# Seven-product groups summed in four PSUM banks, and 40 of 240 convolution taps on ScalarE with accumulating DMAs

## The chip, the cores and the metric

One NeuronCore of a Trainium2 chip runs the whole layer as one program. Its engines run side by side, each through its own list of instructions in order: TensorE (PE, matmuls into PSUM), VectorE (DVE), ScalarE (ACT) and GpSimd (POOL) for elementwise work, SyncE (SP) for issuing DMAs. Semaphores tie them together. An accumulating DMA, one that adds its source to its destination, is issued from POOL. The metric is the device time of one execution in microseconds (us), as the median of a few runs; less is better.

## What is computed

A decoder layer on x of 512 tokens by 2048 channels, f32:

```
h = rms_norm(x, g);  z = h @ W_in            # W_in: 2048 x 7168
a_val, a_glu, a_gate, q, k, v, b_gate = split(z)   # 1024 columns each
u = a_val * sigmoid(a_glu)
u = causal_depthwise_conv(u, w, b)           # 31 taps on 1024 channels
u = silu(layer_norm(u)) @ W_pw + b_pw
y_a = u * silu(a_gate)
o = dilated_window_attention(rms(q), rms(k), v)    # 16 heads of 64, three patterns
y_b = o * silu(b_gate)
out = x + concat(y_a, y_b) @ W_out           # W_out: 2048 x 2048
```

The convolution is, for each channel, `sum_j w[j] u[t - 30 + j] + b`. With d = 30 - j as the distance, there are 31 taps; d = 0 and the bias are one operation, so 30 remain for each of eight blocks of 128 channels: 240 taps.

## The kernel before

**Products.** A weight block is not multiplied in f32. ACT writes a scaled f16 high half and DVE the f16 remainder, and PE takes three f16 matmuls (`tri`, L409 to L413: high by high, high by low, low by high). The weights come in groups of 512 columns (L47): four groups of value and gate columns interleaved ("vg"), then q, k, v, the two gates, the pointwise projection and W_out. Each group has four raw tiles `wf` of 1 MB, loaded by SP into a ring of 8 (`RING`).

**Seven products.** For three groups (`SEVEN`, L53: vg 3, q 0, v 0) a 2 x 2 block product is formed with seven block products in place of eight, in Winograd's form of Strassen's scheme. `input_products` (L1106) writes such a group as a plan: a list of (sub-slot, action). It has 28 sub-slots of one half product each (4 k-tiles x 3 matmuls x 256 columns = 12 matmuls), and PE's matmuls for product n, k-half `pair`, row half m stand at sub-slot 4n + 2 pair + m. The sums of weight blocks s1 to s4 are formed in place in the raw tiles (`add`, L1116): s1 by DVE, s2, s3 and s4 by accumulating DMAs from POOL (`BY_DMA`, L55; the issue is L1122). `hi` (L1126, ACT, recorded at L1128) writes a product's high half `ws` five sub-slots ahead of its product, `lo` (L1130, DVE) the low half four ahead. The sums t1 to t4 of the activations are made beforehand in `sum_x` (L361). Each of the seven results has a PSUM bank of its own while it lives (`lin_ps`, four banks); they are joined on DVE (`first_block`, `joint`, `fifth`, `sixth`, `final`), with two or three results copied to SBUF by ACT first (`copy`, L1178), into tiles `cb`.

**Slots and order.** The order of all engines' instructions is written out by the program, not by a scheduler: a clock `clock[0]` counts slots, `after(n, fn)` puts an action n slots later, and each engine executes what was written to it in that order. A plain group takes 32 slots, 16 products of 4 k-tiles in two halves each; a seven-group uses 28 of its 32. vg 3 has slots 96 to 127, q 0 128 to 159, k 0 160 to 191, v 0 192 to 223, bg 0 224 to 255.

**The convolution.** `conv` (L537) is a generator, pair after pair of channel blocks. For each block ACT writes `cv` = u * w[30] + b (L544), and DVE adds the taps one by one with a fused multiply-add on 128 x 511 down to 128 x 482 elements. `run_conv` (L853) is called every slot: DVE's written work is counted by the helper class `Weighed` (L74; DVE's operations are recorded at its line, L80), a pace (`PACE`, 1230, and 1480 once attention has begun) is taken off per slot, and while the count is below zero the next taps are written. After the last tap the layer norm follows, whose column sums PE does (L568).

**The pool `slots`.** f32 tiles of 128 x 512 (u, cv, cb, gates and others) come from one pool of 35 buffers (`SLOTS`, L31). Who takes a buffer waits until its last users are done, DMAs among them.

**POOL** also computes small per-column scales: `esc` (L424), the scale with which a group's products leave PSUM, and `ss` in `norm_qk` (L470), the norm of q and k for each head.

Of the kernel before, what the change touches and what calls it, by code (L numbers as in the profile page):

```python
# [31 lines left out]
LP = 4  # L32
WARM = 9
# [5 lines left out]
PACE = 1230  # L39
# [15 lines left out]
BY_DMA = ("s2", "s3", "s4")  # L55
SUM_FROM = 58
SUM_STEP = 10
PACE_2 = 1480
# [12 lines left out]
class Weighed:  # L71
# [5 lines left out]
    def __getattr__(self, name):  # L77
        def call(out, src, *args, **kw):
            self.load += START + max(math.prod(a.shape[1:]) for a in (out, src) if hasattr(a, "shape"))
            return getattr(self.engine, name)(out, src, *args, **kw)  # L80
        return call
# [3 lines left out]
def layer(ctx: ExitStack, tc: tile.TileContext, xt, w1, w2, w3, g_in, conv_w, conv_b,  # L85
# [233 lines left out]
    H = S // 2  # L319
# [39 lines left out]
    xn, tx = {}, {}  # L359

    def sum_x(j):  # L361
# [5 lines left out]
        to = tx[j] = (wide if j < 4 else att).tile([P, 4, 2, H], F16, name="tx", tag="wide" if j < 4 else "att")  # L367
        V.tensor_sub(t1, b11, b12)
        V.tensor_sub(t3, b12, b22)
        V.tensor_add(t2, b22, t1)  # L370
        V.tensor_sub(t4, b21, t2)
        both = lambda t: t.rearrange("p (n t) -> p n t", n=2)

        def high():
            for n, t in ((0, t12), (2, t34)):
                A.activation(to[:, n:n + 2, 0], both(t), AF.Copy)

        def low():
            for n, t in ((0, t12), (2, t34)):
                V.tensor_tensor(to[:, n:n + 2, 1], both(t), to[:, n:n + 2, 0], op=OP.subtract)  # L380
# [28 lines left out]
    def tri(ps, a, b, first, last):  # L409
        (ah, al), (bh, bl) = a, b  # L410
        T.matmul(ps, ah, bh, start=first, stop=False)  # L411
        T.matmul(ps, ah, bl, start=False, stop=False)  # L412
        T.matmul(ps, al, bh, start=False, stop=last)  # L413
# [53 lines left out]

    by_head = lambda t: t.rearrange("p (h d) -> p h d", d=DH)

    def norm_qk(store, z, sq, n, to):  # L470
# [4 lines left out]
        def reduce():  # L475
            V.reduce_sum(ss, by_head(sq), axis=AX.X)
            f = 2.0 ** (-2 * QK_SHIFT)
            G.tensor_scalar(ss, ss, f / DH, f * RMS_EPS, op0=OP.mult, op1=OP.add)
            rsqrt(ss)
# [4 lines left out]
        def high():  # L484
            got["hl"] = temp("qhl", F16, [P, 2, S])
            A.activation(got["hl"][:, 0], z, AF.Copy)

        def low():
            hl_t = got["hl"]
            V.tensor_tensor(hl_t[:, 1], z, hl_t[:, 0], op=OP.subtract)  # L490
            for part in range(2):
                if store not in qk:
                    qk[store] = [wide_tile("qk4", [P, 4, S], F16) for _ in range(2)]
                to(qk[store][part], hl_t[:, part])
# [6 lines left out]
    def evac_qk(half_i, t, ps, is_k):  # L501
# [10 lines left out]
        if is_k and ("v", half_i) in SEVEN:  # L512
            n = [4 + 5 * (t > 0), 10 + 2 * t + 2 * (t > 0), 11 + 2 * t + 2 * (t > 0), 13 + 2 * t + 2 * (t > 0)]
        norm_qk(("k" if is_k else "q", half_i), z, sq, n,
                lambda to, src: nc.sync.dma_start(to[:, :, t * P:(t + 1) * P], src, transpose=True))
# [20 lines left out]

    def conv():  # L537

        for i0 in range(0, 8, 2):
            while i0 + 1 not in u:  # L540
                yield 1
            for i in (i0, i0 + 1):
                cv[i] = slot("cv")
                A.activation(cv[i], u[i], AF.Identity, scale=cw[:, i, TAPS - 1:TAPS], bias=cb[:, i:i + 1])  # L544
            yield 2
            for j in range(TAPS - 2, -1, -1):
                d = TAPS - 1 - j
# [151 lines left out]
    def two_heads(pair):  # L699
# [9 lines left out]
        def scores(tiles):  # L709
# [9 lines left out]
            for i in order:  # L719
                w = WIDTH[i]  # L720
                for n, (q, k) in enumerate(((0, 0), (0, 1), (1, 0))):
                    for a, rows in enumerate(halves):
                        T.matmul(ps[i, a], qk["q", hf][q][rows, p4, i * P:w], qk["k", hf][k][rows, p4, :w], start=n == 0, stop=n == 2)  # L723
# [126 lines left out]
    convolution = conv()  # L850
    wait = [0, False]

    def run_conv():  # L853

        pace = PACE_2 if 0 < min(at_pair.values(), default=0) <= clock[0] else PACE
# [249 lines left out]

    def input_products(i0):  # L1106
# [5 lines left out]
        def block(name, pair):  # L1112
            b = PLACE.get(name, name)
            return raw[i0 + 2 * pair + (b[2] == "2")][:, :, H * (b[1] == "2"):][:, :, :H]

        def add(name, pair):  # L1116
            if name == "s1":
                V.tensor_tensor(block("a11", pair), block("a22", pair), block("a11", pair), op=OP.subtract)
            else:
                x, to = SUMS[name]  # L1120
                if name in BY_DMA:
                    nc.gpsimd.dma_start(block(to, pair), block(x, pair), accum_op=OP.add)  # L1122
                else:
                    V.tensor_tensor(block(to, pair), block(to, pair), block(x, pair), op=OP.add)
# [5 lines left out]
        def lo(name, pair):  # L1130
# [3 lines left out]
            for j in range(4):  # L1134
                mine = ("s2", "s4") if j % 2 else ("s1", "s3")
                if all((n, j // 2) in done for n in mine) and all(m in free for m in range(j)) and j not in free:
# [3 lines left out]
                    after(MEASURE, lambda j=j: measure(i0 + j + RING))  # L1140

        def x_part(name, pair, k):

            if name[0] == "t":
                t = tx[4 * pair + k][:, int(name[1]) - 1]
# [4 lines left out]
        order = [("p1", "a11", "b11"), ("u", "a22", "t4"), ("x", "a12", "b21"), ("p7", "s3", "t3"), ("p5", "s1", "t1"),  # L1150
                 ("p6", "s2", "t2"), ("z", "s4", "b22")]
        u_first = group != SEVEN[0]
        if u_first:
            order[:2] = order[1::-1]

        def product(n, pair, m):
            to, w, x = order[n]
            if (pair, m) == (0, 0):
                bank[to] = lin_ps.tile([P, 2, H], F32, name="ps_l", tag="ps_l")
            ps, ms = bank[to][:, m], slice(m * P, (m + 1) * P)  # L1160
            for k in range(KU):
                t, xs = weights[w, pair], x_part(x, pair, k)
                first, last_ = pair == m == k == 0, pair == m == 1 and k == KU - 1
                if by_token:
                    tri(ps, [x[:, ms] for x in xs], (t[:, 0, k], t[:, 1, k]), first, last_)
                else:
                    tri(ps, [t[:, j, k, ms] for j in range(2)], xs, first, last_)
# [10 lines left out]
        def copy(name):  # L1178
            t = got[name] = slot("cb")
            A.activation(t, bank.pop(name).rearrange("p m t -> p (m t)"), AF.Copy, scale=e["p"])  # L1180
# [274 lines left out]
```

## Time and profile before

| | |
|---|---|
| median of 3 runs | 817.66 us (817.63 to 818.33) |
| span of the profiled execution | 815.8 us |
| PE busy | 807.9 us, 99% |
| DVE busy | 707.1 us, 87% |
| ACT busy | 553.6 us, 68% |
| POOL busy | 138.1 us, 17% |
| granted TensorE clock | 0.999 |
| moved by DMA | 125.62 MB, mean 154 GB/s |

A row of the groups reads: line, engine, operation, output tile <- input tiles, shapes, count | busy us, mean ns of one | idle time of the engine just before, and who released it. A row of waits reads: engine, tile and line <- the releaser: us in total, times, longest us. A DMA row gives count, KB each and the median us from issue to landing. The profile was taken from one execution, and the time of a run also holds what lies outside the span, 1.9 us between this span and the median.

### The profile page before, as it was taken

The numbers are of one execution on the slowest core, as the hardware profiler recorded it, in microseconds if no ns is written. First come the engines' busy times: TensorE is split into PE (matmuls) and PEld (weight loads), VectorE is DVE, ScalarE is ACT, GpSimd is POOL, SyncE is SP. The second block draws the span as 40 slices with busy tenths as digits, with TensorE's granted clock in tenths as the row PEclk, the third lists the DMA queues.
The fourth block names the chain that finished last, engine by engine and source line by source line (L and its number), as shares of the span: only waits on it lengthen the run. The fifth ranks groups of instructions, "written<-read, shape, count | busy, mean of one in ns | idle before, by whom it ended". The sixth has DMA issues, their size and how long they took to land.

```text
span 815.8 us, 13495 instructions
## 1 busy us (share of the span) xinstructions
PE 807.9 (99%) x5271; PEld 500.6 (61%) x5271; DVE 707.1 (87%) x1181; ACT 553.6 (68%) x778; POOL 138.1 (17%) x159
## 2 busy tenths in 40 slices
PE   9999999999999999999999999999999999999998
PEld 6887645888646864444444444444444444788887
DVE  6768999889888989999999988996677798998985
ACT  6667687567656678677756748487688858766540
POOL 0001020413223500004112010010110002412420
PEclk9999999999999999999999999999999999999999
DMA  9953343995675862537473632536343477578752
GB/s 341 344 215 102 105 110 98 132 279 113 261 143 114 156 252 98 122 104 174 136 181 100 172 105 86 134 104 168 104 117 104 136 236 234 116 176 189 130 104 66
DMA packets 98625, 125.62 MB, mean 154 GB/s; under 512 B 62720, under 2 KB 83968, under 8 KB 89344
## 3 DMA queue, kind: packets, MB, share of 16 engines
q1 hardware_dynamic: 80800, 107.38, 41.9%
q0 software_dynamic: 17472, 17.30, 14.9%
q8 instruction: 41, 0.67, 0.3%
q14 instruction: 24, 0.20, 0.1%
q10 hardware_dynamic: 288, 0.07, 0.0%
HBM read 88.56 MB, written 4.19 MB: 114 GB/s over the span
## 4 chain that ended last, share of the span: by engine, by line
PE 69%; DVE 19%; ACT 5%; issue 3%; DMA 3%; POOL 1%; SPq 0%; ACTq 0%; DVEq 0%; POOLq 0%
PE ps_l L411 17%; PE ps_l L412 17%; PE ps_l L413 16%; PE ps_l L879 10%; DVE cv L80 6%; DVE wl L80 3%; DVE ws L80 3%; ACT junk L190 2%; PE ps_s L413 2%; PE ps_s L411 2%; PE ps_s L412 2%; PE ps_s L723 2%; PE ps_o L763 2%; DMA wf<-w_dram 1%; DVE cb L80 1%
## 5 line engine op out<-in xcount | busy, mean ns | idle before, releaser
L80 DVE SCALAR_TENSOR_TENSOR cv<-u,cw,cv 128x511 f32<-128x511 f32 (+14 forms) x240 | 162.2, 728 | 0.4 <-ACT cv L544 0.4
L190 ACT ACTIVATE junk<-wf 128x2048 uint8<-128x2048 f32 x68 | 129.2, 1900 | 3.5 <-DMA wf<-w_dram 3.1
L411 PE MATMUL ps_l<-x,wh 128*128 128x512 f16 x320 | 121.4, 379 | 0.3 <-DVE glu L80 0.3
L413 PE MATMUL ps_l<-x,wl 128*128 128x512 f16 x320 | 121.3, 379 | 0.0
L412 PE MATMUL ps_l<-x,wh 128*128 128x512 f16 x320 | 121.3, 379 | 0.0
L299 ACT ACTIVATE wh<-wf,ws 128x2048 f16<-128x2048 f32 x44 | 87.7, 1993 | 49.0 <-PE ps_l L412 49.0
L80 DVE SCALAR_TENSOR_TENSOR wl<-wf,ws,wh 128x2048 f16<-128x2048 f32 x45 | 105.6, 2347 | 13.0 <-ACT wh L299 13.0
L411 PE MATMUL ps_l<-wh,x 128*128 128x512 f16 x256 | 97.1, 379 | 0.0
L412 PE MATMUL ps_l<-wl,x 128*128 128x512 f16 x256 | 97.1, 379 | 0.0
L413 PE MATMUL ps_l<-wh,x 128*128 128x512 f16 x256 | 97.0, 379 | 0.0
L80 DVE SCALAR_TENSOR_TENSOR ws<-wf,ws 128x1024 f16<-128x1024 f32 x70 | 89.0, 1278 | 7.5 <-ACT ws L1128 4.9
L411 PEld LDWEIGHTS <-wh 128*128 128x128 f16 x480 | 47.0, 98 | 55.4 <-issue 3.5
L413 PEld LDWEIGHTS <-wl 128*128 128x128 f16 x480 | 46.9, 98 | 53.6 <-DVE wl L80 0.4
L412 PEld LDWEIGHTS <-wh 128*128 128x128 f16 x480 | 46.9, 98 | 50.4 <-issue 0.7
L879 PE MATMUL ps_l<-xr,wr 128*128 128x512 f32 x288 | 69.7, 397 | 0.1
L204 POOL TENSOR_SCALAR ws<-ws 128x1 f32<-128x1 f32 x22 | 10.7, 485 | 341.8 <-DVE ws L80 313.0
L879 PEld LDWEIGHTS ps_l<-xr,wr 128*128 128x128 f32 x288 | 54.1, 189 | 13.8 <-ACT xr L338 1.0
L413 PEld LDWEIGHTS <-x 128*128 128x128 f16 x352 | 34.4, 98 | 32.8 <-issue 1.5
L411 PEld LDWEIGHTS <-x 128*128 128x128 f16 x352 | 34.4, 98 | 32.4 <-issue 1.9
L412 PEld LDWEIGHTS <-x 128*128 128x128 f16 x352 | 34.4, 98 | 30.6 <-issue 0.5
L946 ACT ACTIVATE ws<-wf,ws 128x1024 f16<-128x1024 f32 x28 | 32.1, 1147 | 28.7 <-PE ps_l L413 9.4
L1128 ACT ACTIVATE ws<-wf,ws 128x1024 f16<-128x1024 f32 x42 | 46.4, 1138 | 6.1 <-PE ps_l L413 3.9
(250 smaller groups left out, 1823.3 us busy)
## 6 DMA issues: line engine op xcount, KB each, us to landing
wf<-w_dram SPq DMA_DIRECT2D x72, 1024.0 KB, 5.2
wf<-wf POOLq DMA_DIRECT2D x30, 512.0 KB, 6.5
x<-xt_dram SPq DMA_DIRECT2D x16, 256.0 KB, 6.7
res<-xt_dram SPq DMA_DIRECT2D x8, 512.0 KB, 6.5
out_dram<-res SPq DMA_DIRECT2D x15, 256.0 KB, 2.2
wf<-w_dram SPq DMA_DIRECT2D x7, 512.0 KB, 7.2
wf<-wf POOLq DMA_DIRECT2D x6, 256.0 KB, 6.3
qk<-qhl SPq DMA_TRANSPOSE x40, 3.0
```

Of the source, the lines that this page charges most:

```text
L80: return getattr(self.engine, name)(out, src, *args, **kw)
L190: A.activation(junk[:, :n], src, AF.Square, scale=scale, accum_out=acc)
L204: G.tensor_scalar(scale, scale, 1e-30, 2.0 ** (-2 * top), op0=OP.max, op1=OP.mult)
L299: A.activation(parts[i][0], raw[i], AF.Copy, scale=wscale[units[i][3:]][0])
L411: T.matmul(ps, ah, bh, start=first, stop=False)
L412: T.matmul(ps, ah, bl, start=False, stop=False)
L413: T.matmul(ps, al, bh, start=False, stop=last)
L723: T.matmul(ps[i, a], qk["q", hf][q][rows, p4, i * P:w], qk["k", hf][k][rows, p4, :w], start=n == 0, stop=n == 2)
L763: T.matmul(po[rows, i * P:(i + 1) * P], vs[hf][j // 2][:, j % 2, 2 * p4 + a, vp * DH:(vp + 1) * DH], got["t", a][:, pp * (ALL // P) + FROM ...
L879: T.matmul(banks[group, m], wt[:, a, m * P:(m + 1) * P], xk[b], start=k == 0 and a == b == 0, stop=k == KC - 1 and a == 1)
L946: A.activation(t[:, 0], block(name), AF.Copy, scale=wscale["wa", g][0])
L1128: A.activation(t[:, 0], block(name, pair), AF.Copy, scale=wscale[group][0])
```

## The change

**Seven products.** The order of the products is new, and results that are only ever added are summed in one PSUM bank by PE itself. `ORDER` names the bank (A to D), the weight block or sum and the activation block or sum of each product. Bank A is read out by ACT after p1, after s2's and after s3's product and never closed between; B is read after s1's and after s4's. So ACT makes five copies a group (three before) and DVE four joining operations (seven before). s1 is now formed by DMA and s3 by DVE; there are 18 DMAs in the three groups as before. A raw tile's halves come free in another order, and the loads and measures that follow move with it. The activation sums change sign in places, and their f16 tiles are shared out over two pools.

**Taps.** For the channel pairs 2 and 4 (`STAGED`) the taps d = 1 to 10 of both blocks, 40 taps in all, leave DVE. ACT multiplies u by the tap's weight into a new tile `tap` of the pool `slots`; a slot later POOL issues an accumulating DMA that adds `tap` to `cv` (256 KB, rows of 2,044 bytes and less). The generator `stages` writes one such tap every 3 slots from slot 92 on, except while q 0 runs: 11 taps from slot 95 to 127, the rest of pair 2 from 160 to 185, pair 4 from 190 to 250. `conv` does the remaining taps of these pairs on DVE afterwards.

**Paces and small things.** `PACE` 1200 and `PACE_2` 1360; `Weighed` counts small operations lower and large ones 4% higher. In `norm_qk` one operation per head group moves from POOL to DVE, and high and low half are transposed by one DMA (32 on SP, 40 before).

```diff
-BY_DMA = ("s2", "s3", "s4")
-PACE = 1230
+STAGED = (2, 4)
+BY_SUMS = 10
+STEP = 3
+STAGE_FROM = 92
+PACE = 1200
-PACE_2 = 1480
+PACE_2 = 1360
...
+    def begin_cv(i):
+        cv[i] = slot("cv")
+        A.activation(cv[i], u[i], AF.Identity, scale=cw[:, i, TAPS - 1:TAPS], bias=cb[:, i:i + 1])
+
+    def stage(i0):
+
+        for i in (i0, i0 + 1):
+            begin_cv(i)
+        yield STEP
+        for d in range(1, BY_SUMS + 1):
+            for i in (i0, i0 + 1):
+                t = slot("tap")
+                A.activation(t[:, d:], u[i][:, :S - d], AF.Copy, scale=cw[:, i, TAPS - 1 - d:TAPS - d])
+                after(1, lambda: nc.gpsimd.dma_start(cv[i][:, d:], t[:, d:], accum_op=OP.add))
+                yield STEP
+        staged[i0] = clock[0] + 8
...
+            while i0 in STAGED and clock[0] < staged.get(i0, 10 ** 9):
+                yield 1
+            for d in range(1 + (i0 in STAGED) * BY_SUMS, TAPS):
...
-    wait = [0, False]
+    convolution, by_sums = conv(), stages()
+    wait = [0, False, STAGE_FROM]
     def run_conv():
+        if clock[0] >= wait[2] and ("q", 0) != at_group[0]:
+            wait[2] = clock[0] + next(by_sums, 10 ** 9)
...
+    ORDER = (("A", "a11", "b11"), ("C", "a12", "b21"), ("B", "s1", "t1"), ("A", "s2", "t2"), ("D", "a22", "t4"),
+             ("A", "s3", "t3"), ("B", "s4", "b22"))
...
-        order = [("p1", "a11", "b11"), ("u", "a22", "t4"), ("x", "a12", "b21"), ("p7", "s3", "t3"), ("p5", "s1", "t1"),
-                 ("p6", "s2", "t2"), ("z", "s4", "b22")]
...
+        def joint(to, name, other, by="p"):
+            got[to] = got.pop(other)
+            V.scalar_tensor_tensor(got[to], flat(name), e[by], got[to], op0=OP.mult, op1=OP.add)
+            bank.pop(name)
...
+        plan = [(2, scales_of), (4, lambda: copy("p1", "A")), (8, lambda: joint("11", "C", "p1")),
+                (17 if kind == "v" else 9, lambda: out("11")), (12, lambda: copy("p5", "B")), (16, lambda: copy("u2", "A")),
+                (20, lambda: (copy("u", "D", "n"), bank.pop("D"))), (24, lambda: copy("nw", "A", "n")), (24, lambda: joint("21", "A", "u", "n")),
+                (25, fourth), (25, lambda: out("21")), (26, lambda: out("22")), (28, lambda: joint("12", "B", "u2")),
+                (29, lambda: out("12"))]
...
+                 for n, name, pair in ((-8, "s1", 0), (-7, "s1", 1), (-1, "s2", 0), (0, "s2", 1),
+                                       (8, "s3", 0), (10, "s3", 1), (8, "s4", 0), (9, "s4", 1))]
```

Two places of the order. The first is ACT in v 0, before: `ws` are high halves of weights, `cb` copies of products out of PSUM, `qhl` high halves of normed k; what a row waits for stands in brackets, DMASW for a DMA issued by POOL, DMAHW by SP, and the name of an engine for that engine.

```order
L1128 ACTIVATE ws_2625<-wf_2111,ws_2342 128x1024 [waits PE_49,Activation_49]
L486 ACTIVATE qhl_2640<-z_2502 128x512 [waits DVE_49]
L1180 ACTIVATE cb_2645<-ps_l_2576 128x512 [waits PE_49]
L1128 ACTIVATE ws_2664<-wf_2147,ws_2342 128x1024 [waits Activation_49]
L1128 ACTIVATE ws_2704<-wf_1978,ws_2342 128x1024 [waits DMASW4_49,PE_49,Activation_49]
L1180 ACTIVATE cb_2719<-ps_l_2648 128x512 [waits PE_49]
L486 ACTIVATE qhl_2736<-z_2523 128x512 [waits DVE_49]
L1128 ACTIVATE ws_2738<-wf_2113,ws_2342 128x1024 [waits DMASW5_49,Activation_49]
```

The same place in the change, from slot 193 on:

```order
L562 ACTIVATE tap_2645<-u_1331,cw_95 128x511 [waits DMASW2_49,Activation_49]
L1172 ACTIVATE ws_2680<-wf_2079,ws_2407 128x1024 [waits DMASW7_49,PE_49]
L498 ACTIVATE qhl_2694<-z_2547 128x4x128 [waits DVE_49]
L1222 ACTIVATE cb_2699<-ps_l_2628 128x512 [waits DMASW5_49,PE_49,Activation_49]
L562 ACTIVATE tap_2702<-u_1279,cw_95 128x510 [waits DVE_49]
L1172 ACTIVATE ws_2720<-wf_2142,ws_2407 128x1024 [waits DMASW1_49]
L1172 ACTIVATE ws_2758<-wf_2079,ws_2407 128x1024 [waits DMASW3_49,PE_49]
L562 ACTIVATE tap_2760<-u_1331,cw_95 128x510 [waits DMASW6_49,Activation_49]
L498 ACTIVATE qhl_2793<-z_2573 128x4x128 [waits DVE_49]
L1172 ACTIVATE ws_2796<-wf_2142,ws_2407 128x1024 [waits DMASW4_49,PE_49]
L562 ACTIVATE tap_2812<-u_1279,cw_95 128x509 [waits DMASW7_49,Activation_49]
```

A tap stands between each two or so of the high halves. Before, a copy `cb` waited for PE alone, and the only DMAs that ACT waited for were the sums of weight blocks ahead of their `ws`; in the change three of the four taps here and the copy wait for a DMA issued by POOL as well.

The second is POOL from the first groups' sums to q 0's, where L1168 issues the sums of weight blocks (`wf`) and L563 the taps:

```order
L563 DMA cv_1282<-tap_1690 128x507 [waits DMASW4_49,DMASW0_49,Activation_49]
L563 DMA cv_1284<-tap_1741 128x507 [waits DMASW5_49,DMASW1_49,Activation_49]
L1168 DMA wf_942<-wf_942 128x4x256 [waits DMASW6_49,DVE_49]
L563 DMA cv_1282<-tap_1794 128x506 [waits DMASW0_49,Activation_49]
L1168 DMA wf_1107<-wf_1107 128x4x256 [waits DMASW7_49,DVE_49]
L430 TENSOR_TENSOR esc_1843<-wi_1350,xinv_127 128x1
L1215 TENSOR_SCALAR nesc_1845<-esc_1843 128x1 [waits Pool_49]
L1168 DMA wf_1014<-wf_942 128x4x256 [waits DMASW2_49,DVE_49]
```

And before at the same place:

```order
L1122 DMA wf_941<-wf_941 128x4x256 [waits DMAHW6_49,DMAHW1_49]
L1122 DMA wf_1107<-wf_1107 128x4x256 [waits DMAHW1_49,DMAHW0_49]
L1122 DMA wf_1014<-wf_941 128x4x256 [waits DMAHW7_49,DMASW6_49,DVE_49]
L1122 DMA wf_1177<-wf_1107 128x4x256 [waits DMAHW1_49,DMASW7_49,DVE_49]
L424 TENSOR_TENSOR esc_1811<-wi_1341,xinv_127 128x1
L1175 TENSOR_SCALAR nesc_1813<-esc_1811 128x1 [waits Pool_49]
```

Three tap DMAs now stand ahead of `esc`; the one of tap_1794 waits for the DMA that last added to the same cv_1282.

165 lines of the change are left out of this document (75 added, 90 removed).

## The prediction

> **What bounds the kernel now.** I read the page's busy times first, then PE's own waits, then busy time by stretches, and last the rows of the operations that the change adds or drops.
>
> ```profile
> span 815.8 us, 13495 instructions
> PE 807.9 (99%) x5271; PEld 500.6 (61%) x5271; DVE 707.1 (87%) x1181; ACT 553.6 (68%) x778; POOL 138.1 (17%) x159
> PE ps_l L412 <- DVE ws L80: 1.8, 2, 1.1
> PE ps_s L146 <- POOL wz L143: 1.0, 1, 1.0
> PE ps_s L568 <- DVE lnacc L80: 0.8, 1, 0.8
> PE ps_l L411 <- ACT ws L1128: 0.4, 1, 0.4
> PE ps_l L411 <- DVE glu L80: 0.3, 1, 0.3
> ```
>
> PE is busy for 807.9 of 815.8 us, and the change takes no matmul away (PE's list of instructions has 9,775 rows in both programs). So a gain can only come out of 7.9 us, of which the start (1.0 us for L146) and the tail belong to no edit. The rows that the change can touch are three: PE waits for DVE's and ACT's weight halves `ws` (1.8 + 0.4 us), for `lnacc` of the layer norm (0.8 us), and for `glu` (0.3 us). What PE lost in each stretch stands in the next view (columns: stretch, length, then busy us of PE, PEld, DVE, ACT, POOL, the granted clock, the DMA share):
>
> ```profile
> core 0: us, PE busy (x) PEld busy (x) DVE busy (x) ACT busy (x) POOL busy (x), PEclk, DMA share, GB/s
> 184.00:212.00 28.00, 28.00 (x259) 25.07 (x258) 25.99 (x32) 17.28 (x18) 7.94 (x6) 1.00 0.58 145
> 240.00:260.00 20.00, 19.34 (x114) 10.87 (x112) 17.60 (x25) 8.24 (x10) 4.42 (x4) 1.00 0.58 113
> 260.00:280.00 20.00, 18.41 (x166) 16.19 (x166) 19.96 (x26) 11.71 (x16) 14.12 (x12) 1.00 0.74 113
> 280.00:300.00 20.00, 20.00 (x157) 14.69 (x156) 16.92 (x23) 14.60 (x16) 0.00 (x0) 1.00 0.83 285
> 300.00:540.00 240.00, 240.00 (x1463) 112.11 (x1462) 230.91 (x423) 168.22 (x252) 29.14 (x36) 1.00 0.48 129
> 540.00:560.00 20.00, 19.21 (x88) 8.53 (x87) 18.70 (x34) 16.38 (x29) 2.79 (x3) 1.00 0.58 154
> ```
>
> PE idles 0.66 + 1.59 = 2.25 us from 240 to 280, in the seven-product group of v0, where DVE is busy 19.96 of 20 us: DVE is the bound there. Another 0.79 us is lost at 540 to 560, in the layer norm, which waits for the convolution on DVE. From 300 to 540 PE loses nothing, though DVE is busy for 231 of 240 us. So the most that a lighter DVE can bring is about 2.25 + 0.79 + 0.3 = 3.3 us.
>
> **The change part by part.**
>
> ```profile
> L80 DVE SCALAR_TENSOR_TENSOR cv<-u,cw,cv 128x511 f32<-128x511 f32 (+14 forms) x240 | 162.2, 728 | 0.4 <-ACT cv L544 0.4
> L80 DVE SCALAR_TENSOR_TENSOR ws<-wf,ws 128x1024 f16<-128x1024 f32 x70 | 89.0, 1278 | 7.5 <-ACT ws L1128 4.9 <-ACT ws L946 2.6
> L1128 ACT ACTIVATE ws<-wf,ws 128x1024 f16<-128x1024 f32 x42 | 46.4, 1138 | 6.1 <-PE ps_l L413 3.9 <-DVE wf L80 1.1 <-ACT ws L1128 0.9
> L1180 ACT ACTIVATE cb<-ps_l,esc x6: 667/678/687, 144.1 to 196.5; 128x512 f32<-128x512 f32 x6
> L80 DVE TENSOR_TENSOR cb<-cb x6: 680/688/692, 172.6 to 294.3; 128x512 f32<-128x512 f32 x6
> L80 DVE SCALAR_TENSOR_TENSOR cb<-ps_l,esc,cb x8: 732/744/749, 155.3 to 215.9; 128x512 f32<-128x512 f32 x8
> L478 POOL TENSOR_SCALAR ss<-ss 128x8 f32<-128x8 f32 x16 | 8.1, 509 | 110.6 <-DVE ss L80 110.6
> L1122 POOL DMA_DIRECT2D wf<-wf x18 | 23.8, 1425 | 31.5 <-DVE ws L80 24.7 <-DMA wf<-wf 5.7 <-issue 1.0
> ```
>
> *DVE.* 40 taps of 0.728 us leave it: 29.1 us. Each of the three groups evacuates with 4 DVE operations in place of 7 (three are products added on the way out, 0.744 us, one an addition, 0.688): about 2.1 us a group, 6.3 in all. 16 operations of norm_qk on 8 columns come over from POOL, where they take 0.509 us: at most 8.1 us, at least nothing, and I take 2.4. So DVE loses about 33 us (27 to 35). PE can gain at most the 3.3 us above from it; the rest meets PE's full stretches.
>
> *ACT.* 40 scaled copies of 128 x 511: no such row with a scale from SBUF; the nearest are 0.678 (from PSUM) and, for f16, 0.62; I take 0.65, 26 us. Two more copies a group: 6 x 0.68 = 4.1 us. As a sum it fits: ACT is busy for 8.24 + 11.71 of the 40 us in v0, where about 6 us are added. What matters is the order.
>
> *The order in v0.* A slot of the plan is one product's half, 12 matmuls. From 184 to 212 us 259 matmuls take 28.00 us, so a slot is 12 x 0.108 = 1.30 us. A product's high half is written by ACT (1.138 us) five slots ahead and its low half by DVE (1.278 us) four slots ahead, 5.2 us. The spare time is 5.2 - 1.28 = 3.9 us: so far may ACT fall behind before PE stands still.
>
> ACT's order in the change has, between these halves, taps and copies that wait for a DMA to land. The 35 buffers of the pool `slots` are as many as before, but four more are held from early on (two pairs of `cv` begun ahead) and each tap takes one until its DMA has landed. So in v0 a new tap gets the buffer of a tap sent shortly before. Followed through the rows, tap_2645 waits for the landing of tap_2603's DMA, the copy of p1 into cb_2699 for that of tap_2645, tap_2760 for the DMA issued three slots earlier, and so on at slots 203, 206 and 210: six landings one after another on an in-order ACT, from tap_2603 at slot 191 to the copy at slot 210. A seven-group uses seven of every eight slot numbers, so the plan gives this 17 x 1.30 = 22.1 us. Behind them on ACT stand the high halves, behind those DVE's low halves, and PE waits for both.
>
> What a landing costs is in no row for this form (128 rows of 2,044 bytes added into SBUF). The nearest (the third row is of all 36 accumulates of `wf`, the fourth of the two issued between 764 and 775 us, one of 512 and one of 256 KB, the fifth of the two issued between 157 and 160 us):
>
> ```profile
> out_dram<-res SPq DMA_DIRECT2D x15, 256.0 KB, 2.2
> wf<-wf POOLq DMA_DIRECT2D x30, 512.0 KB, 6.5
> wf<-wf POOLq DMA_DIRECT2D x6, 256.0 KB, 6.3
> DMA to landing us min/median/max: 5.0/6.5/20.3
> DMA to landing us min/median/max: 5.0/6.5/8.0
> DMA to landing us min/median/max: 14.9/17.6/20.3
> 255.00:277.00 22.00, 19.75 (x177) 16.93 (x175) 20.75 (x27) 13.13 (x17) 16.66 (x15) 1.00 0.67 105
> 157.00:178.00 21.00, 21.00 (x195) 18.80 (x193) 19.71 (x26) 12.58 (x15) 2.87 (x3) 1.00 1.10 283
> ```
>
> A tap is 256 KB. Its lower bound is the plain transfer of that size, 2.2 us; its upper bound the median of the accumulates of that size, 6.3. I take 5.0, the quickest accumulate of all, because it adds like those, and because the DMA engines are busy for 0.67 of v0's 22 us, so that some of the six go undisturbed. Each step is then 0.65 (tap) + 5.0 + 0.2 (semaphores, an estimate from the few tenths of "issue" between rows) = 5.85 us, six of them 35.1 us: 13.0 us behind the plan, less 3.9 us spare: PE stalls for 9.1 us. With 2.2 us the six take 18.3 us and nothing shows. With 6.3 they take 42.9, 20.8 behind, and 16.9 us show. DVE's own stall there (2.25 us) is gone in each case, for DVE loses 2.1 us of evacuation there and the taps of the stretch. Net: +6.8 us, between -2.3 and +14.6.
>
> *The order in q0.* POOL issues in order. In the change the tap of slot 128 waits for the landing of tap 121's DMA, and behind it stand s2's second DMA and `esc`, which ACT needs at slot 132 for the first copy.
>
> ```profile
> 183.17 0.67 ACT L1180 ACTIVATE cb<-ps_l,esc 128x512 f32<-128x512 f32 x1
> L424 POOL TENSOR_TENSOR esc<-wi,xinv x12: 180/730/1931, 116.7 to 607.3; 128x1 f32<-128x1 f32 x12
> ```
>
> The first copy ran at 183.17 us before. From 157 to 178 us the DMA engines are full (1.10 in the row above, 283 GB/s, weights for the most part), and the accumulates issued at its start landed after 14.9 and 20.3 us. A landing behind that burst, then four POOL issues of 1.43 us and `esc` of 0.73 put the copy at 184.6 to 186.6 us (178 + 6.6 to 8.6), up to 3.4 us late, and ACT's weight halves behind it. I take 1.6 us of PE; between 0 (3.9 us spare cover it) and 6 (one more accumulate of 8 us or so crawls).
>
> *The rest.* Taps in k0 and bg0, and POOL's 40 x 1.43 = 57 us of issues, lie beside PE; POOL has its 17% share and loses 16 operations there. If that cover were gone, the queue behind them would be the same small operations and DMAs as in q0. In bg0, behind v0, ACT gets some 5 us more on 14.60 of 20 us (280 to 300), spread over 40 us, and its taps wait for older landings: nothing. The other seven-group, vg3, has only 11 taps ahead of q0 and a free pool: nothing. The layer norm's 0.79 us goes, because DVE reaches its convolution end with 33 us less work: -0.8; if DVE's pace (1200 and 1360 in place of 1230 and 1480) spends that spare time, 0. The transposes of q and k fall from 40 to 32 on SP, which no PE wait names: nothing.
>
> Sum: 815.8 + 6.8 + 1.6 - 0.8 = 823.4 us of span. The median of the runs, 817.66, lies 1.9 us above this span, so **825 us**.
>
> **Rivals.**
>
> *A, faster: no landing binds.* If a landing takes up to 3.8 us, six steps take at most 27.9 us, 5.8 behind the plan, of which 3.9 is spare and ACT, idle for half of 240 to 280, makes up the rest. Then v0's 2.25 and the norm's 0.8 us go: 812.8 us, and 814.7 us as a run; with 1.2 us left in q0, 815.9. For it: the trace names a full DVE as the cause of v0's stalls, and a plain transfer of that size takes 2.2 us. Against: no accumulate landed in under 5.0. The Trainium skill (DMA: Bandwidth & Descriptors, "Anatomy of one DMA — SWDGE (gpsimd) path") fits a DMA of this path at 2.0 us plus its bytes by 436 KB a us; by that a tap would land in 2.6 us and six steps take 20.7 us, inside the plan. The trace doesn't agree for accumulates: by that fit the 512-KB ones would land in 3.2 us, and their median is 6.5.
>
> *B, the two even out.* Landings of 3.8 to 4.6 us put the chain 6 to 10.6 us behind; 2 to 6 us show, and the 2.25 + 0.8 us that go pay for them. With q0 at 0 to 1.6 that gives 816 to 819.3 as a run.
>
> *C, slower by more: the queue in front of each tap decides.* s2's and s4's 512-KB DMAs use POOL's queue in v0 as well. If each tap lands at the median, 6.3 us, v0 loses 14.6 net, with q0 and the norm 15.4: 831.2 us of span, 833 as a run. For it: two of the accumulates issued close together landed 14.9 and 20.3 us later. Against: that was in the full stretch, and v0's is at 0.67.
>
> *D, the reordered products alone set a new wait.* The first raw buffer comes free at slot 16 of a group, not 12, so its refill and measure come 4 x 1.30 = 5.2 us later; if the next group's weights were late by that, a group loses up to 5.2 us less 3.9 spare, three groups 4 us: 815.8 + 4 - 3.1 + 1.9 = 818.6, which is B's time. PE waits nowhere for a load in this trace, which speaks against it.
>
> **How the numbers follow.** What a measurement here can tell from no change is about 0.2%, 1.6 us. The forecast (landings from 4.6 to 5.7 us, 819.3 to 829) gets 0.44; A 0.26; B with D 0.16; C 0.14. The likeliest's own time is 825 us, its own range 819.3 to 829. As A and the forecast are of both signs, the range reaches down into A and up into C: 813.7 to 832, which leaves out the lowest part of A and half of C. Faster 0.26, same 0.16, slower 0.58.
>
> **What would show it.** Right: PE's waits between 240 and 300 us grow to 7 to 12 us and name `ws` by ACT L1172; ACT's `tap` and `cb` rows wait there for a DMA of `cv<-tap`, about 3 us each; those DMAs land in 4.5 to 5.5 us; near 180 us ACT's copy waits for POOL's `esc`. Wrong: PE idles under 1 us from 240 to 280 and the taps land in under 4 us (A), or PE's waits stay with DVE's low halves although DVE is no longer full, and then the cause is another than ACT's order. The layer norm's wait at 546 us is to be gone; if it stays, the pace decides it and not DVE's load.

## The result: 4.1% slower, more than four times the loss that was forecast

The changed kernel takes 850.88 us (median of 4 runs, 849.31 to 852.19), the kernel before 817.64 in the same comparison: a ratio of 1.0406, 95% interval 1.0392 to 1.042. The forecast was 825 us, with a range up to 832. The sign was right, the size was not. The profiled execution took 852.08 us and has a span of 850.3.

The busy times of the changed kernel and PE's longest waits:

```profile
PE 817.1 (96%) x5271; PEld 505.3 (59%) x5271; DVE 680.4 (80%) x1148; ACT 580.5 (68%) x824; POOL 159.6 (19%) x183
PE ps_l L417 <- ACT cb L1222: 7.6, 1, 7.6
PE ps_o L802 <- DMA pt<-hl: 7.4, 2, 4.7
PE ps_l L417 <- ACT ws L1172: 4.8, 2, 3.9
```

DVE did become lighter, from 707.1 to 680.4 us (26.7 us, against the 27 to 35 that were forecast), and PE stands still more. It is also busy for longer, 817.1 us against 807.9, with the same matmuls. Both are seen by stretch (the columns are those of the prediction's table; the third last is the granted clock):

```profile
180.00:200.00 20.00, 16.52 (x151) 14.37 (x149) 14.06 (x17) 13.07 (x15) 8.04 (x8) 1.00 1.06 167
200.00:220.00 20.00, 19.14 (x164) 15.85 (x162) 17.48 (x24) 12.10 (x14) 4.40 (x5) 1.00 0.63 234
260.00:280.00 20.00, 15.09 (x126) 12.51 (x124) 13.32 (x21) 10.86 (x15) 12.44 (x10) 0.89 0.70 106
280.00:300.00 20.00, 13.08 (x108) 11.10 (x107) 10.94 (x12) 7.84 (x11) 7.15 (x9) 0.84 1.12 124
300.00:320.00 20.00, 18.14 (x120) 12.51 (x120) 10.19 (x11) 11.43 (x14) 2.59 (x3) 0.84 0.97 311
320.00:340.00 20.00, 19.51 (x104) 8.74 (x103) 14.57 (x31) 18.40 (x25) 3.39 (x4) 1.00 0.52 117
340.00:360.00 20.00, 17.38 (x81) 7.58 (x79) 17.64 (x34) 19.97 (x33) 6.75 (x8) 1.00 0.70 173
360.00:380.00 20.00, 12.65 (x103) 6.91 (x101) 13.12 (x21) 8.34 (x11) 2.55 (x4) 0.74 0.99 129
540.00:560.00 20.00, 20.00 (x149) 9.73 (x148) 20.00 (x29) 12.82 (x15) 1.45 (x2) 1.00 0.67 172
```

Four losses, less what is gone, make up the difference of the two spans, 34.5 us. PE's idle time is 20 us a row less its busy time:

| place | PE's loss in the change | from |
|---|---|---|
| q0 | 4.3 us | 180 to 220 |
| v0, with the first wait of bg0 | 13.7 us | 260 to 320 |
| the first pair of attention | 10.5 us | 320 to 380 |
| matmuls at a lower clock | 9.2 us | PE busy 817.1 - 807.9 |
| gone from the kernel before | -3.0 us | 2.25 in v0, 0.79 in the layer norm |
| together | 34.7 us | |

**v0 went by the mechanism that was forecast.** ACT in the timeline of the changed kernel (start, duration, engine, line, what; in brackets ACT's idle time before and its releaser), and then POOL in the same stretch:

```profile
265.63 0.72 ACT L562 ACTIVATE tap<-u,cw 128x511 f32<-128x511 f32 x1 [1.46 <-DMA cv<-tap]
273.87 0.60 ACT L1222 ACTIVATE cb<-ps_l 128x512 f32<-128x512 f32 x1 [5.95 <-DMA cv<-tap]
278.88 0.72 ACT L562 ACTIVATE tap<-u,cw 128x510 f32<-128x510 f32 x1 [1.73 <-DMA cv<-tap]
284.55 0.72 ACT L562 ACTIVATE tap<-u,cw 128x509 f32<-128x509 f32 x1 [3.40 <-DMA cv<-tap]
295.61 0.72 ACT L562 ACTIVATE tap<-u,cw 128x509 f32<-128x509 f32 x1 [7.27 <-DMA cv<-tap]
300.02 0.60 ACT L1222 ACTIVATE cb<-ps_l 128x512 f32<-128x512 f32 x1 [1.52 <-DMA cv<-tap]
```

```profile
261.84 0.93 POOL L563 DMA_DIRECT2D cv<-tap  x1 [1.86 <-ACT tap L562]
262.47 2.96 POOL L1168 DMA_DIRECT2D wf<-wf  x2
266.65 0.88 POOL L563 DMA_DIRECT2D cv<-tap  x1 [1.21 <-ACT tap L562]
280.89 3.20 POOL L1168 DMA_DIRECT2D wf<-wf  x2
285.63 0.89 POOL L563 DMA_DIRECT2D cv<-tap  x1 [1.54 <-ACT tap L562]
```

Six landings in a row hold ACT up, 21.3 us together, and they are the six of the prediction, from the tap issued at 261.84 to the copy at 300.02: 38.2 us, where the forecast had 35.1. The two long waits, 5.95 and 7.27 us, are for the taps issued at 266.65 and 285.63, each just behind two 512-KB sums of weight blocks. The chain doesn't end there: two more copies of v0 and two taps behind it wait for landings, 10.1 us together from 305 to 323.

### The profile page after: what moved, and what is told of

Same layout as the page of the kernel before. It is cut to its first block, busy times and chain, and to the rows that moved or that the text cites. A ratio compares the mean times of both kernels' runs of the same rounds, so it can differ in the third digit from the quotient of the medians.

```text
span 850.3 us, 13553 instructions
## 1 busy us (share of the span) xinstructions
PE 817.1 (96%) x5271; PEld 505.3 (59%) x5271; DVE 680.4 (80%) x1148; ACT 580.5 (68%) x824; POOL 159.6 (19%) x183
## 4 chain that ended last, share of the span: by engine, by line
PE 76%; DMA 8%; ACT 5%; issue 5%; DVE 3%; POOL 3%; SPq 0%; ACTq 0%; POOLq 0%; DVEq 0%
PE ps_l L417 19%; PE ps_l L419 19%; PE ps_l L418 19%; PE ps_l L921 10%; DMA cv<-tap 6%; PE ps_o L802 2%; PE ps_s L419 2%; PE ps_s L417 2%; PE ps_s L418 2%; PE ps_s L761 2%; ACT junk L195 2%; DMA pt<-hl 1%; POOL cv L563 1%; POOL ss L173 1%; DVE wl L85 1%
## 5 line engine op out<-in xcount | busy, mean ns | idle before, releaser
L85 DVE SCALAR_TENSOR_TENSOR cv<-u,cw,cv 128x501 f32<-128x501 f32 (+14 forms) x200 | 135.7, 725 | 2.9 <-ACT cv L552 2.9
L209 POOL TENSOR_SCALAR ws<-ws 128x1 f32<-128x1 f32 x22 | 10.6, 482 | 256.3 <-DVE ws L85 227.2
L563 POOL DMA_DIRECT2D cv<-tap x40 | 36.8, 928 | 104.4 <-ACT tap L562 78.6
L417 PEld LDWEIGHTS <-x 128*128 128x128 f16 x352 | 34.4, 98 | 32.9 <-issue 2.5
L419 PEld LDWEIGHTS <-x 128*128 128x128 f16 x352 | 34.5, 98 | 31.7 <-issue 0.5
L418 PEld LDWEIGHTS <-x 128*128 128x128 f16 x352 | 34.5, 98 | 30.1
L988 ACT ACTIVATE ws<-wf,ws 128x1024 f16<-128x1024 f32 x28 | 32.1, 1147 | 28.2 <-PE ps_l L419 9.2
```

What stands on the lines that cost most here:

```text
L209: G.tensor_scalar(scale, scale, 1e-30, 2.0 ** (-2 * top), op0=OP.max, op1=OP.mult)
L417: T.matmul(ps, ah, bh, start=first, stop=False, skip_group_check=more)
L418: T.matmul(ps, ah, bl, start=False, stop=False, skip_group_check=more)
L419: T.matmul(ps, al, bh, start=False, stop=last, skip_group_check=more)
L563: after(1, lambda: nc.gpsimd.dma_start(cv[i][:, d:], t[:, d:], accum_op=OP.add))
L988: A.activation(t[:, 0], block(name), AF.Copy, scale=wscale["wa", g][0])
```

## The experiments

The theory after the result: the taps are all of the loss, through landings that ACT and POOL wait for in order, and the new products gain a little. The rivals: the new products are to blame; ACT's work on the taps is; or the pool's shortage alone.

### 1. The products alone

```diff
-STAGED = (2, 4)
+STAGED = ()
-PACE = 1200
+PACE = 1230
-PACE_2 = 1360
+PACE_2 = 1480
```

> The seven-products as in the change, no taps by DMA, the paces of before (1230 and 1480). If the loop of landings through the buffers of the pool is the cause, there is no loop here: PE's waits for ws in q0 and v0 are under 3 us together, the clock stays at 0.999, and the time is 812 to 819 us. If the new order of the products is itself the cause (raw tiles free later, other waits), q0 and v0 keep 10 us or more of PE's waits and the time is above 828 us.

Measured: 815.15 us (7 runs), ratio 0.9971, interval 0.996 to 0.9982. That is faster than the kernel before by 2.4 us, and the best of all that was run. PE's one wait of note that the start doesn't have, and v0:

```profile
PE ps_s L606 <- DVE lnacc L85: 1.0, 1, 1.0
260.00:280.00 20.00, 20.00 (x186) 17.92 (x184) 18.92 (x28) 12.26 (x16) 12.22 (x9) 1.00 0.80 111
```

The 1.59 us that PE lost here before are gone: DVE is at 18.92 of 20 us and was at 19.96. DVE's load alone doesn't settle that stall, though: experiment 3 has DVE at 18.84 in this stretch and PE still waits 1.5 us for a low half of DVE's. The new products, with the small things that came along, aren't to blame for the loss; they bring 2.4 of the 3 us that the prediction's rival A hoped for.

### 2. The taps alone

The old products with the taps, at the paces of the change (`stage`, `stages` and `conv` as in the change's diff):

```diff
-PACE = 1230
+STAGED = (2, 4)
+BY_SUMS = 10
+STEP = 3
+STAGE_FROM = 92
+PACE = 1200
-PACE_2 = 1480
+PACE_2 = 1360
...
-    convolution = conv()
+    convolution, by_sums = conv(), stages()
```

> The kernel before with the 40 taps by ACT and DMA alone: the old seven-products, the paces of the change (1200 and 1360). If the taps are all of the loss, q0, v0 and the first pair of attention lose as in the change or, with three cb copies a group in place of five, somewhat less: 838 to 855 us. If the loss needs the new products too (more buffers of slots in v0, five copies waiting for them), 818 to 830 us.

Measured: 870.55 us, 1.065 (1.0634 to 1.0666), worse than expected. So the taps cost 53 us with the old products and 35.7 (850.88 - 815.15) with the new. PE waits in this run for high halves by ACT, 15.9 us, and for low halves by DVE, 10.3 us. The rest of the change (the new products, the weights in `Weighed`, `norm_qk`, the transposes) doesn't only cost nothing, it softens the taps. Which part of it does so, and how, isn't shown.

### 3. ACT's work without the landings

```diff
-                after(1, lambda: nc.gpsimd.dma_start(cv[i][:, d:], t[:, d:], accum_op=OP.add))
+                pass
```

> The change, with ACT writing all 40 tap tiles as before but none of them sent, so that the 40 taps are missing from the convolution. No landing is waited for and POOL issues nothing for the taps; ACT's load is that of the change. If the landings are the cause, PE's stalls in q0 (5 us), v0 (13 us) and the first pair of attention (13 us) are all gone and the clock stays at 0.999: 813 to 819 us. If it is ACT's extra 28 us of taps that comes too late, the stalls in v0 and in attention stay and the time is above 830 us.

Measured: 816.48 us, 0.9985 (0.9975 to 0.9994). All 40 copies are made on ACT, nothing is sent, and the loss is gone (0.7 us remain in q0, and in v0 1.6, as many as in the kernel before):

```profile
180.00:200.00 20.00, 19.31 (x179) 17.15 (x177) 16.36 (x22) 15.02 (x19) 6.36 (x5) 1.00 0.47 70
260.00:280.00 20.00, 18.44 (x168) 16.23 (x167) 18.84 (x27) 13.93 (x19) 13.73 (x9) 1.00 0.72 103
340.00:360.00 20.00, 20.00 (x145) 9.53 (x140) 19.90 (x44) 11.91 (x21) 1.69 (x3) 1.00 0.31 106
```

ACT's extra work costs little where it comes in time; it is the sending, and what waits for it, that costs 34.4 us (850.88 - 816.48). This run takes away the landings, POOL's issues and the bytes at once, and doesn't part them.

### 4. The sending without the bytes

```diff
-                after(1, lambda: nc.gpsimd.dma_start(cv[i][:, d:], t[:, d:], accum_op=OP.add))
+                after(1, lambda: nc.gpsimd.dma_start(cv[i][:, d:d + 8], t[:, d:d + 8], accum_op=OP.add))
```

> The change, with each of the 40 accumulating DMAs cut to 8 columns of the tap (32 bytes a row in place of some 2,000); the rest of each tap is missing from the convolution. It keeps every wait and every issue, and takes the bytes away. If a landing is mostly a fixed time, it stays at 2.5 to 3.5 us alone, the chain of six in v0 takes 6 x 4 = 24 us of its 22, and v0 loses 0 to 4 us; q0's queue still waits through the burst of weight loads unless small packets pass it: 818 to 832 us. If the bytes are the cost, landings fall under 2.5 us and the time is 813 to 818 us. If they matter not at all, 845 us or more.

Measured: 835.31 us (830.69 to 840.38), 1.0216 (1.0159 to 1.0273), a little above the first of the three cases. The four runs lie far apart: two took 830.7 and 831.5, two 839.2 and 840.4, and the profile is of the slowest, so its stalls stand for the upper pair. From issue to landing (min, median, max of a stretch), first the change at 140 to 152 us with little else on the queue, at 152 to 186 us beside the burst of weight loads, and at 255 to 300 us in v0; then this run at 140 to 152 and at 255 to 300 us:

```profile
DMA to landing us min/median/max: 3.4/3.7/3.9
DMA to landing us min/median/max: 4.6/9.6/12.7
DMA to landing us min/median/max: 3.3/4.2/9.9
DMA to landing us min/median/max: 2.0/2.0/2.0
DMA to landing us min/median/max: 2.1/5.5/8.0
```

Alone, a tap lands after 3.4 us and its first 8 columns after 2.0: a fixed part of 2.0 us and 1.4 us for the bytes. In v0 the bytes matter little, since the short DMAs stand behind the same 512-KB sums and land after up to 8.0 us: PE still loses 10.2 us from 260 to 320 in the profiled run (13.7 in the change; 0 to 4 in v0 were expected). q0, in contrast, is nearly clean here (0.58 us of idle time from 180 to 200): there it was the taps' bytes, among full DMA engines, that made the queue late. The Trainium skill (DMA: Bandwidth & Descriptors, "Anatomy of one DMA — SWDGE (gpsimd) path") has a fixed 2.0 us, and the short taps agree to the tenth. By its fit a tap of 256 KB would land in an estimated 2.6 us; an accumulate of that size took 3.3 at best.

One of the larger stalls of the profiled run, 6.9 us near 351 us, is no landing: PE waits there for ACT's `gate`, and ACT 9.4 us for POOL's scale `esc`. Experiment 6 has the same wait and shows its rows.

### 5. One pair of taps, pair 2 or pair 4

```diff
-STAGED = (2, 4)
+STAGED = (2,)
```

> The change with the taps of pair 2 alone (20 taps, the last near slot 185, all ahead of v0). Loop theory: v0's 13 us, the slow matmuls behind them and the 13 us in the first pair of attention are gone, q0's 5 us stay: 817 to 824 us. If the products are the cause, v0 keeps its stalls and the time stays above 835 us.

Measured: 832.49 us, 1.0181 (1.0166 to 1.0196). v0 and attention behaved as the theory has it: 19.91 of 20 us busy from 260 to 280, no loss from 280 to 560. q0 kept its stall. But the total was 8 us above the range, because of waits that the expectation didn't have:

```profile
600.00:620.00 20.00, 16.55 (x70) 7.87 (x68) 14.27 (x30) 13.26 (x20) 1.96 (x4) 0.86 0.61 165
620.00:640.00 20.00, 15.50 (x124) 7.25 (x124) 14.46 (x27) 14.62 (x21) 1.24 (x3) 0.72 0.10 30
PE ps_l L417 <- ACT u L319: 3.6, 1, 3.6
PE ps_s L398 <- DVE lnacc L85: 2.6, 1, 2.6
```

The paces of 1200 and 1360 let DVE do fewer taps a slot. They fit 40 taps taken away; with 20 put back, the convolution ends too late for the layer norm. This is read from the waits; pair 2 alone at the old paces wasn't run.

```diff
-STAGED = (2, 4)
+STAGED = (4,)
-PACE = 1200
+PACE = 1230
-PACE_2 = 1360
+PACE_2 = 1480
```

> The change with the taps of pair 4 alone (20 taps, slots 190 to 250), at the paces of before, since DVE keeps 20 more taps. Loop theory: q0's stalls are gone or under 1.5 us (no tap ahead of esc on POOL), v0's are as in the change or somewhat less (two cv fewer are held early, so the pool is less tight): 825 to 845 us. If the landing loop needs the pool to be full and two buffers are enough to free it, 814 to 820 us.

Measured: 826.37 us, 1.0105 (1.009 to 1.012). The expectation had the place wrong: with pair 2 out of the list, the generator begins pair 4 at slot 95, and the taps ran from 143 to 258 us. So it is a second look at taps ahead of v0, not at taps in it. q0 lost 2.1 us, v0 1.3, and another 6.4 us went near 615 us, in a wait that experiment 8 has as well.

### 6. The taps of pair 4 moved, or cut

Paused in v0 as they are in q0:

```diff
-        if clock[0] >= wait[2] and ("q", 0) != at_group[0]:
+        if clock[0] >= wait[2] and at_group[0] not in (("q", 0), ("v", 0)):
```

> The change with the taps paused in v0 as they are in q0, so that pair 4 is sent from slot 224 to about 290, in bg0, q1 and the first pair of attention. Loop theory: v0 without stalls over 2 us, q0's 5 us stay. What the later taps do in the first pair of attention is open: if the 13 us lost there come from ACT's lateness out of v0, they go and the time is 818 to 826 us; if they come from taps landing beside the transposes and the weight loads there, they stay or grow: 830 to 845 us.

Measured: 836.39 us, 1.0224 (1.0207 to 1.0241). v0 loses 0.7 us (PE busy for 19.28 us from 260 to 280), so in the change its stalls came with the taps in it. Another 5.9 us and the clock go at 340 us, in one wait for POOL's `esc` (the last two rows are POOL and DVE there):

```profile
PE ps_l L417 <- ACT gate L471: 5.9, 1, 5.9
ACT gate L471 <- POOL esc L430: 9.9, 1, 9.9
340.00:360.00 20.00, 14.14 (x121) 6.43 (x119) 12.29 (x25) 11.96 (x16) 10.84 (x8) 0.83 0.66 130
335.43 10.36 POOL L430 TENSOR_TENSOR esc<-wi,xinv 128x1 f32<-128x1 f32 x1
339.26 6.48 DVE L85 SCALAR_TENSOR_TENSOR cv<-u,cw,cv 128x492 f32<-128x492 f32 x10
```

This is no queue of taps. `esc` begins at 335.43 us, before ACT is ready for it, and then lasts 10.36 us, where the median of its 12 rows is 0.73. It ends at 345.79, and DVE, which has worked without a pause since 327, comes to its first pause at 345.74. The long `esc` of experiments 2 and 4 (12.1 and 12.3 us) end within 0.1 us of such a pause too. So DVE's unbroken row of taps seems to hold POOL's operation up; that is read from these three rows and wasn't tested. Whether the taps' DMAs brought `esc` into that stretch isn't shown either.

Pair 4 alone, but where the change has it:

```diff
-STAGED = (2, 4)
+STAGED = (4,)
-STAGE_FROM = 92
+STAGE_FROM = 187
-PACE = 1200
+PACE = 1230
-PACE_2 = 1360
+PACE_2 = 1480
```

> The change with the taps of pair 4 alone, from slot 190 to 250 where the change has them, at the paces of before. v0 has the same taps, DMAs and ACT work as the change, but two cv fewer are held by then, so that a tap or copy gets a buffer that was let go earlier. Loop theory: ACT's waits for cv<-tap in v0 fall from 17 us to under 6 and PE loses under 4 us there, q0 nothing: 815 to 822 us. If taps in v0 cost as such (ACT's order, the DMAs beside s2 and s4), v0 keeps 8 us or more: 825 us and above.

Measured: 839.64 us, 1.0282 (1.0257 to 1.0306). The total missed the expectation, the place did not. ACT's waits for `cv<-tap` from 258 to 310 us are 7.7 us (23.0 in the change, under 6 expected), and v0 is clean from 260 to 280 while its taps are sent:

```profile
260.00:280.00 20.00, 19.93 (x184) 17.70 (x183) 18.73 (x27) 14.52 (x20) 13.52 (x11) 1.00 1.13 160
280.00:300.00 20.00, 18.50 (x141) 12.51 (x140) 13.72 (x17) 13.90 (x15) 3.93 (x6) 1.00 1.26 222
```

The same 20 taps in the same slots, with two tiles fewer held, hold ACT up far less, although their median landing is longer, 8.2 us. That fits the pool as the link between a landing and ACT. It isn't the pool alone that differs: pair 2's taps are back on DVE, and the paces are the old ones. The loss moves behind v0. The DMA engines are at 1.13 and 1.26, and PE waits for low halves `wl` (8.5 us) and for the transposes `pt` (5.8 us) from 300 to 350 us. Another 6.4 us go near 615 us, as with pair 4 early.

Pair 4 cut to four taps a block, so that no tap is sent after slot 214:

```diff
-    staged = {}
+    staged, by_sums_of = {}, {2: BY_SUMS, 4: 4}
-        for d in range(1, BY_SUMS + 1):
+        for d in range(1, by_sums_of[i0] + 1):
-            for d in range(1 + (i0 in STAGED) * BY_SUMS, TAPS):
+            for d in range(1 + by_sums_of.get(i0, 0), TAPS):
```

> The change with pair 4's taps ended after d = 4 (8 taps, slots 190 to about 214, in place of 20 to slot 250); DVE does the other 12. v0 runs as in the change, and bg0 and the first pair of attention have no taps. If the 13 us lost from 305 to 380 us come from ACT and DVE still being late out of v0, they stay: 840 us or more, with the waits for pt<-hl. If the taps sent there make them (their copies on ACT, their accumulates beside the weight loads and the transposes), PE loses under 3 us from 305 to 380 us while v0 keeps its 13 us. As in the run with pair 2 alone, the low paces may then cost some us in the layer norm near 620 us, which is apart from this.

Measured: 848.19 us, 1.0376 (1.0361 to 1.0392). v0 keeps its 11.4 us from 260 to 300, and the three rows from 320 to 380 us are now at 20.00 of 20:

```profile
360.00:380.00 20.00, 20.00 (x156) 9.68 (x151) 16.82 (x37) 11.57 (x21) 0.58 (x2) 1.00 0.32 106
```

So the 10.5 us in the first pair of attention aren't lateness brought out of v0 alone. They come with the 12 taps that this run doesn't send, all after 302 us. Experiment 3, where the same copies cost nothing there, points to the landings again; late copies without landings weren't run. The total is only 2.7 us better than the change's because the low paces, with 12 taps put back on DVE, lose 7.6 us from 600 to 660 us, and the clock with it, as in experiment 5.

### 7. q0's scale ahead of the taps

```diff
-        plan = [(2, scales_of), (4, lambda: copy("p1", "A")), (8, lambda: joint("11", "C", "p1")),
+        plan = [(-5 if group == ("q", 0) else 2, scales_of), (4, lambda: copy("p1", "A")), (8, lambda: joint("11", "C", "p1")),
```

> The change, with q0's esc and nesc computed seven sub-slots earlier on POOL, ahead of the taps that wait. In the change ACT waited 3.9 us for esc at 184 to 188 us. If esc behind waiting tap DMAs is what makes q0's stall, PE's 5 us there fall to 2 to 3 (s2's second DMA is still behind the taps, and the copy's buffer still waits for a tap's landing at about 185 us): 846 to 849 us as a whole. If s2's DMA alone sets it, q0 stays at 5 us and the time at 851.

In the change, POOL and ACT stand like this at the start of q0:

```profile
172.24 0.88 POOL L563 DMA_DIRECT2D cv<-tap  x1 [5.45 <-ACT tap L562]
185.51 0.91 POOL L563 DMA_DIRECT2D cv<-tap  x1 [2.58 <-DMA cv<-tap]
187.02 0.95 POOL L430 TENSOR_TENSOR esc<-wi,xinv 128x1 f32<-128x1 f32 x1
188.00 0.69 ACT L1222 ACTIVATE cb<-ps_l,esc 128x512 f32<-128x512 f32 x1 [3.90 <-POOL esc L430]
```

The tap of 185.51 waits for the one of 172.24, which took 12.7 us to land, `esc` waits behind it, and the copy for `esc`. Measured: 845.89 us, 1.0347 (1.0332 to 1.0363), 5 us less than the change. PE's idle time from 180 to 220 fell from 4.3 to 3.3 us; the rest of the gain lies in later stretches (attention's two waits for `pt` are 5.4 us in place of 7.4, `cb` 5.2 in place of 7.6), where the cause wasn't separated. `esc` is a part of q0's stall. With it out of the way ACT waits 3.8 us there for sums of weight blocks that stand behind the same taps, which it did not in the change: they are the larger part.

### 8. More pace for the products alone

```diff
-PACE_2 = 1480
+PACE_2 = 1540
```

on top of experiment 1, and then also `PACE = 1260`:

> The seven-products of the change without taps, paces 1230 and 1540 in place of 1480: DVE writes the convolution's taps earlier once attention runs. The run at 1480 left one wait that a pace can move, 1.0 us for the layer norm's sum. If that goes and nothing else comes late, 814.2 us against 815.15; if DVE, at 19 of 20 us there, holds attention up in its place, 815 to 817 us.

> The same with 1260 ahead of attention too: taps come earlier in q0, k0 and v0. v0's ws waits (0.2 us at 1230) may come back, 0.5 to 2 us, as DVE was at 18.9 of 20 us there; the layer norm's 1.0 us is gone: 814 to 816 us.

Measured: 830.88 us, 1.0159 (1.0143 to 1.0174), and 827.21 us, 1.0119 (1.0102 to 1.0136). Both missed by over 10 us. The second run's PE, and ACT, at 580 to 620 us:

```profile
PE ps_l L419 <- DVE wl L85: 3.9, 1, 3.9
PE ps_l L417 <- ACT wh L304: 2.1, 1, 2.1
580.00:600.00 20.00, 20.00 (x96) 9.10 (x95) 7.18 (x15) 19.38 (x31) 3.11 (x2) 1.00 0.16 52
600.00:620.00 20.00, 13.93 (x52) 5.28 (x51) 15.14 (x26) 17.57 (x25) 1.84 (x5) 0.74 0.54 118
```

When the convolution ends earlier, the layer norm's ACT work (`cv`, `u`) falls among the softmax of a pair of heads. ACT, the fourth busy time of a row, is at 19.38 of 20 us there, in an order that mixes the two, and the weight halves come 6 us late. The same two waits, 2.1 and 4.3 us, stand in the two runs with pair 4 alone at the paces 1230 and 1480. That ACT's order is the cause is read from the chain of waits and wasn't tested by itself.

## Why the prediction was wrong

The forecast span was 823.4 us, the profiled one 850.3. The 27 us between them are v0 (4.6 more than its 9.1), q0 (2.7 more than its 1.6), the first pair of attention (10.5 in place of nothing) and the clock (9.2 in place of nothing).

**Right: where the loss begins.** The loop of landings in v0 was read from the order and the pool before any run. The trace shows the six landings that it named, and with the runs without sending (816.48 us) and with v0 paused the stall goes. The landing was set at 5.0 us for each. The six took 3.7, 7.1, 3.4, 4.2, 9.9 and 3.3 us from issue, 5.3 in the mean: the sum was near, but no single landing was like the forecast's, and that two long ones and four short ones gave its mean is luck. What sets them apart is what rival C had named, the queue ahead of each tap. PE lost 13.7 us with bg0's first wait, inside the bounds of 0 to 16.9.

**Mis-sized: q0.** The step "I take 1.6 us of PE", with bounds of 0 and 6, gave 4.3. It counted `esc` alone. The sum of weight blocks behind the same taps is late too, and after `esc` was moved 3.3 us remained.

**Failed: bg0, "its taps wait for older landings: nothing".** This is the step that cost most. In bg0 two taps held ACT up for 6.6 us in such waits, and from 320 to 380 us PE lost 10.5 us. The prediction checked bg0's taps against bg0's own slots and stopped there. The taps run on into the first pair of attention, later than planned, up to 360 us. ACT is at 18.40 and 19.97 of 20 us there. The two transposes `pt` issued at 353.71 and 361.29 us land after 16.1 and 11.5 us, where they took 5.6 to 6.4 in the kernel before; one load of weights and the last three taps (6.1, 13.2 and 10.6 us to land) are in flight with them. Neither the run without sending nor the run with the taps cut loses anything from 320 to 380, although in the second v0 has its stalls. The step that failed is thus the end of the taps: they had landings beside the transposes, and the prediction looked for them only beside bg0.

**Missing: the clock.** The sum priced a stall at its length. The chip took more: 9.2 us of PE's busy time are matmuls at a lower granted clock after the long stalls. Some 6 of them (an estimate from the granted clock of 0.89, 0.84 and 0.84 in the three rows from 260 to 320) stand behind v0's stalls, which the prediction had in its sum; with them its 825 us would have been 831.

**Rival A was half true.** The prediction treated the two halves of the change as one and gave the gain to the lighter DVE. Of the two, the products take 2.4 us away with 3.5 us less DVE work (703.6 in place of 707.1), and the taps take another 23.2 us off DVE for a loss of 35.7 us. Rival A's own condition, no landing that binds, is the run without sending: 816.48 us, not 814.7; v0 keeps 1.6 us of its stall there although DVE is lighter, and q0 loses 0.7. That the products alone come to 815.15 is near its number by another way. The layer norm's 0.8 us did go as forecast.

**Sums that don't follow.** By the prediction's own terms a landing of 4.6 us leaves 10.6 - 3.9 = 6.7 us of stall and gives a run of about 823 us, so the upper end of rival B and the lower end of the forecast's own range should be 823 and not 819.3. POOL's issue of a tap was taken at 1.43 us and took 0.93.

## What to carry to other kernels

A DMA that an in-order engine waits for, through a buffer that is handed round, costs its landing behind everything in its queue, and not only its own bytes: measure it there, and count how many follow one another. Follow a moved piece of work to its last instruction, not to the end of the stage in which it begins. When PE is at 99%, look for the stretch in which the engine to be relieved is full before paying for its relief elsewhere.

## What the hardware showed that was not expected

The clock after a stall. Three stretches of the changed kernel: after a wait of about 4 us, right behind it, and after a wait of 7.6 us. The fourth row is q0 in the run that pauses the taps in v0:

```profile
276.00:283.00 7.00, 5.89 (x30) 4.09 (x30) 6.83 (x9) 3.42 (x5) 7.00 (x6) 0.53 0.38 64
283.00:292.00 9.00, 9.00 (x85) 8.08 (x83) 6.05 (x7) 3.80 (x5) 1.98 (x2) 1.00 1.62 154
300.00:306.00 6.00, 5.33 (x26) 3.68 (x26) 3.08 (x3) 4.24 (x6) 0.89 (x1) 0.50 0.96 265
180.00:200.00 20.00, 18.03 (x150) 15.14 (x149) 14.17 (x17) 13.59 (x17) 7.51 (x8) 0.91 1.09 172
```

After the first wait PE ran 30 matmuls in 7 us where it then runs 85 in 9, at a clock of 0.53, for some 5 us. q0's short stalls behave otherwise. The change and the run of the fourth row, whose order of work up to there is the same, both have two, of 0.9 and 1.1 us, within 2 us near 190, and the change a third of 1.5 us at 194: it stays at 1.00, and the other falls to 0.91 over the 20 us. The Trainium skill (TensorE: Matmul & The Clock Gate, 'Part 1: The HAM clock gate (the "warmup" mystery)') has half the clock after an idle window of about 3.4 us, in a window that runs freely, so that the same kernel can differ from run to run. The two long stalls agree with it. q0's are all shorter than that window, so the page's rule doesn't explain the 0.91; what does stays open. In this kernel a stall of 4 us cost 2 to 3 us beyond its length (some 5 us at half rate).

An accumulate of 256 KB lands after 3.3 us at best, of which 2.0 are there for 4 KB as well, and after 7 to 13 us behind two 512-KB accumulates or beside a burst of weight loads.

The scale `esc` of 128 x 1 on POOL, 0.4 to 0.7 us at the median, took 10.4 to 12.3 us once in each of three runs and ended within 0.1 us of DVE's first pause (experiment 6).
